# A decoder trunk's first layer: the norm's column product on another engine, low parts and sines issued later, the first weights split elsewhere

## The chip, the cores and the metric

The kernel runs on one core of a Trainium2 chip. The metric is the device time of one execution in microseconds (us). The core has TensorE (PE, with its weight loads PEld), VectorE (DVE), ScalarE (ACT), GpSimd (POOL) and SyncE (SP), which here only issues DMA transfers. Each engine works through its own queue in order and waits on semaphores for what others produce.

## What is computed

Two layers of a decoder trunk over 512 tokens and 2048 channels. The part that matters here is the head of a layer: a modulation vector from `c`, an RMS norm of `x`, and one large projection.

```python
for l in range(DEPTH):
    mod = c_act @ ada_w[l] + ada_b[l]
    shift, scale, gate = [m[:, None, :] for m in jnp.split(mod, 3, axis=-1)]
    h = rms_norm(x, norm_g[l]) * (1.0 + scale) + shift
    z = h @ w_in[l]
    ...                      # attention and conv groups from z's columns, cos/sin tables for the rope
    x = x + gate * y
```

## The kernel before

Tokens lie along the free axis; channels along the 128 partitions, in 16 chunks of 128 channels by 512 tokens. All matmuls are fp32 made of two fp32r parts: a value is split into a high part (a rounding cast) and a low part (the difference), and `mm3` (L248 to L251) issues three matmuls, high x high, high x low, low x high. Weights are split by `split_w` (L235): the cast on ScalarE (L242), the difference on the engine that is named (L243; `SENG`, GpSimd). A load of eight 128x128 weight tiles (`load_w`, L228, four buffers "raw") is cut into two such splits of 128x512, each with 5 buffers for high and low.

**The start.** `rope_angles` makes angles on VectorE. `first_x` (L373) loads x and sums its squares: squares on ScalarE, additions on VectorE (the first on GpSimd), and at the end two additions that join three partial sums (L384, L385). `token_rsqrt` (L212 on) sums over channels on TensorE (L194) and takes the inverse root on VectorE in a chain of small steps (L215, L176 to L184), and `token_bc` (L204, L209) spreads it over the partitions. `rope_tables` (L168) takes two sines on ScalarE.

**The modulation.** `Gemv.block(l, b)` (L332) makes 128 columns of the modulation: it loads a 1 MB block of `ada_w` into one of three buffers ("ada") and VectorE multiplies and reduces it (L336, 128x2048). Block j is the shift of chunk j (called shift block j below), block 16 + j its scale (scale block j). `make_gs` (L348, L350) turns the scale into (1 + scale) * norm_g, a 128x1 step on VectorE. `make_h` (L352) then makes h of a chunk in three steps: x * gs * rstd on VectorE (L356), the high part with the shift added on ScalarE (L357), the low part on VectorE (L358).

**Layer 0's order.** `modulated(j)` (L422) is, in the program's order: scale block j (for j = 0 it is done earlier, `EARLY` = 1), L350, shift block j, L356, L357, L358. `chunk` (L397) loads eight weight tiles and gives TensorE 24 matmuls for one chunk of h. There are three passes: chunks 0 to 2 of the first projection (`K1` = 3; the sums in PSUM are then parked, copies L431), 8 chunks of the gate's columns with h 0 to 7 (`KH`; parked too), and chunks 3 to 15 of the first projection. `modulate_to` (L434) keeps h ahead of TensorE: 0.6 chunks of h for each chunk of weights in the second pass, 0.7 in the third. What follows (attention, conv, output, layer 1) is not touched.

**What sets the order.** The program is traced in the order above, and a planner then orders each engine's queue: of the instructions that it believes ready at a time it takes the one that was traced first. `issue_after` puts what a block traces behind one instruction on that engine, `keep_in_program_order` (the GpSimd splits) behind the one before. The DMA queue's order on SP is that of the program in this stage. A load into a buffer waits at the head of SP's queue until the buffer is free, and the loads behind it wait too.

Of the kernel before, what the change touches and what calls it, by code (L numbers as in the profile page):

```python
# [50 lines left out]
def hybrid_trunk(ctx, tc, xT, c, pos, invf, vec, adaT, w_s, w_t, w_kr, w_q, w_kv, w_pw, w_o, outT):  # L51
# [287 lines left out]
    def shift(l, j):  # L339
        return mods[l][:, j:j + 1]  # L340
# [11 lines left out]
    def make_h(l, j, x, rstd, h=None, tk=slice(0, S)):  # L352

        h = r4("h") if h is None else h
        hi, lo, x = h[:, 0, tk], h[:, 1, tk], x[:, tk]
        V.scalar_tensor_tensor(out=x, in0=x, scalar=gs(l, j), in1=rstd, op0=ALU.mult, op1=ALU.mult)  # L356
        A.activation(out=hi, in_=x, func=AF.Identity, bias=shift(l, j))  # L357
        bc_ins[1] = V.scalar_tensor_tensor(out=lo, in0=x, scalar=shift(l, j), in1=f(hi), op0=ALU.add,  # L358
                                           op1=ALU.subtract)
        return h  # L360
# [12 lines left out]
    def first_x():  # L373
        xs = []
        accs = [ms("acc") for _ in range(3)]
        for j in range(0, KC, 2):
            t = r4f("x")
            nc.sync.dma_start(out=t, in_=xT[j:j + 2].rearrange("k p t -> p k t"))
            for e in range(2):

                acc = accs[2] if j < 4 else accs[e]
                square_sum(acc, t[:, e], j + e if j < 4 else j - 4, nc.gpsimd if j < 4 else V)
                xs.append(t[:, e])
        V.tensor_add(out=accs[0], in0=accs[0], in1=accs[2])  # L384
        V.tensor_add(out=accs[0], in0=accs[0], in1=accs[1])  # L385
        return xs, accs[0]

    def layer(l, xs, rstd, rpsum):
# [5 lines left out]

        tags = [t for t in ("mm", "up", "s", "cv", "pz") for _ in range(NB[t])]

        def chunk(tiles, src, hj, start, stop):  # L397
            raw = load_w(src, 8, P)
            for q in (0, 4):
                hi, lo = split_w(raw[:, q:q + 4], SENG)  # L400
                for n in range(4):
                    mm3(tiles[q + n], hi[:, n], lo[:, n], hj[:, 0], hj[:, 1], start, stop)

# [15 lines left out]

        h, part = [], [None] * H  # L420
        if l == 0:
            def modulated(j):  # L422
                if j >= EARLY:
                    scale0(j)
                g.block(0, j)
                h.append(make_h(0, j, xs[j], rstd if j else rpsum[0]))

            def park(tiles, where):
                for n in range(8):
# [1 line left out]
                    (A.copy if n % 2 else V.tensor_copy)(out=p, in_=tiles[n])  # L431
                    yield p

            def modulate_to(m):  # L434
                while len(h) < min(int(m), KC):
                    if len(h) < NI:
                        with tc.issue_after(rstd_ins.ins):
                            modulated(len(h))
                    else:
                        modulated(len(h))  # L440

            first = [psum(t, "z") for t in tags]
            for j in range(K1):
                modulate_to(j + 1)
                chunk(first, w_first(j), h[j], j == 0, j == K1 - 1)
            held = list(park(first, lambda n: ms("held") if n < 2 else f2("held", "held", 6, sp)))
            mg = [psum(t, "z") for t in tags]
            for j in range(KH):
                modulate_to(max(j + 1, K1 + MR0 * (j + 1)))
                chunk(mg, w_t[l, 0:H, :, j, :].rearrange("a p b -> p a b"), h[j], j == 0, j == KH - 1)  # L450
            part = list(park(mg, lambda n: ms("part")))
            first = [psum(t, "z") for t in tags]
            for j in range(K1, KC):
                modulate_to(max(j + 1, K1 + MR0 * KH + MR * (j + 1 - K1)))
                chunk(first, w_first(j), h[j], j == K1, j == KC - 1)
            krw = kr_weights()
            for n in range(8):
# [570 lines left out]

    def scale0(j):
        g.block(0, 16 + j)  # L1030
        make_gs(0, j)

    for j in range(EARLY):
        scale0(j)
    rstd0 = ms("rstd")
    state = (xs, rstd0, [token_rsqrt_bc(acc, D, rstd0)])
    rope_tables()
    rstd_ins = bc_ins[0]
    for l in range(DEPTH):
        state = layer(l, *state)  # L1040
# [61 lines left out]
```

## Time and profile before

| | us |
|---|---|
| median of 3 runs | 1679.31 |
| lowest, highest | 1675.61, 1680.39 |
| the profiled execution | 1681.96 |
| its span | 1680.2 |
| TensorE busy in the span | 1587.6 |
| VectorE busy | 1211.6 |
| ScalarE busy | 687.5 |
| GpSimd busy | 640.5 |

The profile is one execution. Its span runs from the first instruction to the last; the execution's own time is 1.8 us longer. Times below are us from the span's start, the mean of one instruction in ns. In the name of a step, `ada` is a modulation block, `mod` the modulation columns, `h` a chunk of h, `hi` and `lo` the parts of weights, `raw` loaded weights, `z` the projection's sums in PSUM. The engine named behind an arrow is the one that released a waiting instruction.

### The profile page before, as it was taken

The page shows a single profiled execution, that of the slowest core. Times are in us where ns is not written, and L with a number is a line of the kernel's source. Part 1 is how long each engine was busy: PE and PEld are TensorE (multiplying, and loading weights), DVE is VectorE, ACT ScalarE, POOL GpSimd, SP SyncE. Part 2 cuts the span into 40 slices and gives each one's busy share as a digit, 9 for nine tenths or more (in the row PEclk, how much of TensorE's full clock was granted, in tenths as well). Part 3 has the DMA queues.
Part 4 walks back from the last instruction along what each step waited for, and adds up shares of the span by engine and source line. Part 5 has one row for each costly group of instructions (what it writes and reads, how often), then busy time and mean ns, then how long its engine had stood idle before and what let it go on. Part 6 is the DMA issues. An engine that isn't in the chain of part 4 may idle for free.

```text
span 1680.2 us, 20681 instructions
## 1 busy us (share of the span) xinstructions
PE 1587.6 (94%) x7350; PEld 1299.3 (77%) x7350; DVE 1211.6 (72%) x2008; ACT 687.5 (41%) x1284; POOL 640.5 (38%) x440
## 2 busy tenths in 40 slices
PE   4988999999999999998899899999999999999999
PEld 2766778887878888877678678888787878888888
DVE  8898897888899645665469856677887786555553
ACT  4222455554544345321223355544544443532221
POOL 3565633424233445554535546243343326200000
PEclk9999999999999999999999999999999999999999
DMA  8878323222232732797885633233223335337672
GB/s 299 281 282 290 132 86 97 68 84 82 76 108 84 238 100 89 254 331 268 307 293 181 267 97 104 72 98 97 75 71 97 105 128 181 93 110 253 237 261 88
DMA packets 82890, 271.53 MB, mean 162 GB/s; under 512 B 10721, under 2 KB 21729, under 8 KB 70241
## 3 DMA queue, kind: packets, MB, share of 16 engines
q1 hardware_dynamic: 82786, 270.20, 47.5%
q8 instruction: 58, 0.95, 0.2%
q14 instruction: 46, 0.38, 0.1%
HBM read 257.55 MB, written 12.62 MB: 161 GB/s over the span
## 4 chain that ended last, share of the span: by engine, by line
PE 55%; DVE 27%; DMA 6%; ACT 6%; issue 3%; POOL 1%; SPq 0%; POOLq 0%; DVEq 0%; ACTq 0%
DVE ada L336 7%; DVE cv L547 7%; PE wo L251 4%; PE z L251 4%; PE z L249 4%; PE z L250 4%; PE wo L249 4%; PE wo L250 4%; PE cg L251 3%; PE cg L249 3%; PE cg L250 3%; DMA ada<-in_adaT_dram 3%; DMA raw<-in_w_o_dram 3%; PE pw L250 2%; PE pw L251 2%
## 5 line engine op out<-in xcount | busy, mean ns | idle before, releaser
L243 POOL TENSOR_TENSOR lo<-raw,hi 128x512 fp32r<-128x512 f32 x380 | 575.6, 1530 | 690.1 <-ACT hi L242 680.9
L242 ACT CAST hi<-raw 128x512 fp32r<-128x512 f32 (+1 forms) x512 | 306.4, 612 | 559.3 <-PE wo L250 152.9
L547 DVE SCALAR_TENSOR_TENSOR cv<-u,lvec,cv 128x512 f32<-128x512 f32 x464 | 348.7, 751 | 7.2
L249 PE MATMUL z<-h,hi 128*128 128x512 f32 (+1 forms) x782 | 308.2, 399 | 17.0 <-ACT h L357 10.9
L251 PE MATMUL z<-h,lo 128*128 128x512 f32 (+1 forms) x782 | 308.7, 395 | 8.6 <-POOL lo L243 8.5
L250 PE MATMUL z<-h,hi 128*128 128x512 f32 (+1 forms) x782 | 307.2, 393 | 0.7 <-DVE h L358 0.7
L336 DVE CUSTOM_DVE_ANT_0 ada<-ada,cb,avec 128x2048 f32<-128x2048 f32 x96 | 251.2, 2618 | 27.3 <-DMA ada<-in_adaT_dram 27.3
L249 PE MATMUL wo<-cat,hi 128*128 128x512 f32 (+1 forms) x544 | 207.8, 382 | 11.0 <-ACT hi L242 10.9
L251 PE MATMUL wo<-cat,lo 128*128 128x512 f32 (+1 forms) x544 | 207.9, 382 | 4.2 <-POOL lo L243 3.8
L250 PE MATMUL wo<-cat,hi 128*128 128x512 f32 (+1 forms) x544 | 207.0, 381 | 0.0
L249 PEld LDWEIGHTS z<-h,hi 128*128 128x128 f32 x782 | 150.0, 193 | 49.2 <-ACT h L357 13.4
L251 PEld LDWEIGHTS z<-h,lo 128*128 128x128 f32 x782 | 149.9, 192 | 43.3 <-POOL lo L243 13.5
L250 PEld LDWEIGHTS z<-h,hi 128*128 128x128 f32 x782 | 149.8, 192 | 29.5 <-DVE h L358 1.8
L243 DVE TENSOR_TENSOR lo<-raw,hi 128x512 fp32r<-128x512 f32 (+1 forms) x132 | 85.5, 660 | 80.3 <-ACT hi L242 80.1
L249 PEld LDWEIGHTS wo<-cat,hi 128*128 128x128 f32 x544 | 103.8, 191 | 32.0 <-ACT hi L242 13.1
L251 PEld LDWEIGHTS wo<-cat,lo 128*128 128x128 f32 x544 | 103.6, 190 | 26.3 <-POOL lo L243 6.8
L250 PEld LDWEIGHTS wo<-cat,hi 128*128 128x128 f32 x544 | 103.8, 191 | 19.0
L249 PE MATMUL cg<-h,hi 128*128 128x512 f32 x256 | 101.0, 394 | 0.0
L251 PE MATMUL cg<-h,lo 128*128 128x512 f32 x256 | 99.8, 390 | 0.0
L250 PE MATMUL cg<-h,hi 128*128 128x512 f32 x256 | 99.8, 390 | 0.0
L780 ACT ACTIVATE pr<-pr,smx,sc 128x128 f32<-128x128 f32 (+1 forms) x64 | 41.9, 654 | 110.3 <-DVE smx L779 110.2
L251 PE MATMUL mg<-h,lo 128*128 128x512 f32 x192 | 76.3, 397 | 2.3 <-POOL lo L243 2.3
(265 smaller groups left out, 2469.4 us busy)
## 6 DMA issues: line engine op xcount, KB each, us to landing
ada<-in_adaT_dram SPq DMA_DIRECT2D x96, 1024.0 KB, 5.5
raw<-in_w_t_dram SPq DMA_DIRECT2D x120, 512.0 KB, 3.9
raw<-in_w_o_dram SPq DMA_DIRECT2D x64, 512.0 KB, 5.8
raw<-in_w_s_dram SPq DMA_DIRECT2D x32, 512.0 KB, 6.4
raw<-in_w_pw_dram SPq DMA_DIRECT2D x16, 512.0 KB, 3.6
raw<-in_w_q_dram SPq DMA_DIRECT2D x24, 256.0 KB, 2.7
x<-in_xT_dram SPq DMA_DIRECT2D x8, 512.0 KB, 7.3
kf<-kfd SPq DMA_DIRECT2D x16, 256.0 KB, 3.9
```

What stands on the lines that cost most here:

```text
L242: A.copy(out=hiv, in_=rawv)
L243: i = eng.tensor_tensor(out=lov, in0=rawv, in1=f(hiv), op=ALU.subtract)
L249: T.matmul(out=ps, lhsT=whi, rhs=mhi, start=start, stop=False)
L250: T.matmul(out=ps, lhsT=whi, rhs=mlo, start=False, stop=False)
L251: T.matmul(out=ps, lhsT=wlo, rhs=mhi, start=False, stop=stop)
L336: V.tensor_tensor_reduce(out=t, in0=t, in1=self.cb, scale=1.0, scalar=vv(l, "ada_b", b), op0=ALU.mult, op1=ALU.add, accum_out=mods[l][:, b ...
L547: V.scalar_tensor_tensor(out=box[-1], in0=u[:, k:k + S], scalar=w, in1=box[0], op0=ALU.mult, op1=ALU.add)
L780: A.activation(out=pr[:, :n], in_=pr[:, :n], func=AF.Exp, scale=scl, bias=nb, accum_out=sums)
```

## The change

- `make_gs` for layer 0 becomes an activation on ScalarE: gs = scale * norm_g + norm_g, with norm_g as both the scale and the bias column.
- The low part of a chunk (L358) is no longer traced right behind its high part. It is held in `pending` and traced behind the next chunk's scale block: either when the next chunk is modulated, or at once where the chunk is the last that was made and TensorE is about to use it; then the next scale block is begun first (`begin(j + 1)`), except for chunk 0.
- The sines are traced behind the high part of chunk 0 instead of before the layer.
- The first chunk's weights are split on VectorE instead of GpSimd.
- The addition L384 is traced behind the fifth load of x instead of at the end.

```diff
@@ first_x
-        V.tensor_add(out=accs[0], in0=accs[0], in1=accs[2])
+            if j == 8:
+                V.tensor_add(out=accs[0], in0=accs[0], in1=accs[2])
         V.tensor_add(out=accs[0], in0=accs[0], in1=accs[1])
@@ layer
-        def chunk(tiles, src, hj, start, stop):
+        def chunk(tiles, src, hj, start, stop, eng=SENG):
...
-                hi, lo = split_w(raw[:, q:q + 4], SENG)
+                hi, lo = split_w(raw[:, q:q + 4], eng)
...
+            pending, begun = [], [EARLY]
+
+            def begin(j):
+                if j < KC and j == begun[0]:
+                    begun[0] += 1
+                    scale0(j)
+
+            def settle():
+                while pending:
+                    pending.pop()()
+
             def modulated(j):
-                if j >= EARLY:
-                    scale0(j)
+
+                begin(j)
+                settle()
                 g.block(0, j)
-                h.append(make_h(0, j, xs[j], rstd if j else rpsum[0]))
+                t, r = r4("h"), rstd if j else rpsum[0]
+                hi, lo, x = t[:, 0], t[:, 1], xs[j]
+                V.scalar_tensor_tensor(out=x, in0=x, scalar=gs(0, j), in1=r, op0=ALU.mult, op1=ALU.mult)
+                hi_ins[0] = A.activation(out=hi, in_=x, func=AF.Identity, bias=shift(0, j))
+                pending.append(lambda: V.scalar_tensor_tensor(out=lo, in0=x, scalar=shift(0, j), in1=f(hi),
+                                                              op0=ALU.add, op1=ALU.subtract))
+                h.append(t)
...
-            def modulate_to(m):
+            def modulate_to(m, j):
...
+                if j == len(h) - 1 and pending:
+                    if j:
+                        begin(j + 1)
+                    settle()
...
             for j in range(K1):
-                modulate_to(j + 1)
-                chunk(first, w_first(j), h[j], j == 0, j == K1 - 1)
+                modulate_to(j + 1, j)
+                if j == 0:
+                    with tc.issue_after(hi_ins[0].ins):
+                        rope_tables()
+                chunk(first, w_first(j), h[j], j == 0, j == K1 - 1, SENG if j else V)
...
     def scale0(j):
         g.block(0, 16 + j)
-        make_gs(0, j)
+        n = vv(0, "norm_g", j)
+        A.activation(out=gs(0, j), in_=gs(0, j), func=AF.Identity, scale=n, bias=n)
...
-    rope_tables()
```

## Rows read from the trace of the kernel before

**Rows 1.** Table by stretch: busy us (count) of PE, PEld, DVE, ACT, POOL, clock, DMA, GB/s.
```profile
104.00:190.60 86.60, 78.86 (x322) 62.07 (x323) 75.32 (x64) 24.31 (x44) 52.61 (x29) 0.96 0.69 251
120.00:130.00 10.00, 10.00 (x46) 8.29 (x45) 9.17 (x6) 1.75 (x3) 6.50 (x5) 1.00 0.71 252
```

**Rows 2.** Chain of waits in the first 420 us, shares by engine and line.
```profile
by line: DVE ada L336 18.3%; DVE cv L547 7.2%; PE z L251 5.1%; issue 5.1%; PE z L249 5.0%; PE z L250 4.8%; DVE x L356 4.2%; DVE mod L350 3.2%; DVE h L358 2.4%; ACT h L357 2.3%; DVE lat L586 2.0%; PE st L194 1.6%; DVE pr L776 1.4%; DMA raw<-
```

**Rows 3.** Groups of DVE, 43.6 to 185.9 us: count | busy us, mean ns | idle before.
```profile
L336 DVE CUSTOM_DVE_ANT_0 ada<-ada,cb,avec 128x2048 f32<-128x2048 f32 x28 | 81.1, 2896 | 0.0
L356 DVE SCALAR_TENSOR_TENSOR x<-x,mod,rstd 128x512 f32<-128x512 f32 x14 | 19.5, 1393 | 0.4
L350 DVE SCALAR_TENSOR_TENSOR mod<-mod,avec 128x1 f32<-128x1 f32 x14 | 13.7, 978 | 0.4
```

**Rows 4.** Groups of POOL, 43.6 to 188 us, the weights' low parts.
```profile
L243 POOL TENSOR_TENSOR lo<-raw,hi 128x512 fp32r<-128x512 f32 x44 | 87.4, 2013 | 61.8 <-ACT hi L242 61.8
```

**Rows 5.** Timeline of DVE: start, duration, step [idle before, releaser].
```profile
110.78 0.15 DVE L350 SCALAR_TENSOR_TENSOR mod<-mod,avec 128x1 f32<-128x1 f32 x1
...
135.99 0.75 DVE L358 SCALAR_TENSOR_TENSOR h<-x,mod,h 128x512 fp32r<-128x512 f32 x1 [0.79 <-ACT h L357]
136.66 2.34 DVE L336 CUSTOM_DVE_ANT_0 ada<-ada,cb,avec 128x2048 f32<-128x2048 f32 x1
...
139.04 1.09 DVE L350 SCALAR_TENSOR_TENSOR mod<-mod,avec 128x1 f32<-128x1 f32 x1
140.17 1.74 DVE L356 SCALAR_TENSOR_TENSOR x<-x,mod,rstd 128x512 f32<-128x512 f32 x1
141.83 2.34 DVE L336 CUSTOM_DVE_ANT_0 ada<-ada,cb,avec 128x2048 f32<-128x2048 f32 x1
...
144.97 0.75 DVE L358 SCALAR_TENSOR_TENSOR h<-x,mod,h 128x512 fp32r<-128x512 f32 x1 [0.79 <-ACT h L357]
```

**Rows 6.** Timeline of POOL in the same stretch (x6, x4: splits in one run).
```profile
111.06 12.92 POOL L243 TENSOR_TENSOR lo<-raw,hi 128x512 fp32r<-128x512 f32 x6 [3.82 <-ACT hi L242]
...
138.00 3.36 POOL L243 TENSOR_TENSOR lo<-raw,hi 128x512 fp32r<-128x512 f32 x2 [5.88 <-ACT hi L242]
145.52 7.57 POOL L243 TENSOR_TENSOR lo<-raw,hi 128x512 fp32r<-128x512 f32 x4 [4.16 <-ACT hi L242]
```

**Rows 7.** Waits, 20 to 200 us: total us, times, longest.
```profile
DVE h L358 <- ACT h L357: 11.9, 15, 0.8
```

**Rows 8.** Timeline of DVE at the start, chunk 0.
```profile
22.33 0.69 DVE L384 TENSOR_TENSOR acc<-acc,acc 128x512 f32<-128x512 f32 x1
...
23.66 2.34 DVE L336 CUSTOM_DVE_ANT_0 ada<-ada,cb,avec 128x2048 f32<-128x2048 f32 x1
...
26.05 1.09 DVE L350 SCALAR_TENSOR_TENSOR mod<-mod,avec 128x1 f32<-128x1 f32 x1
...
27.13 1.23 DVE L176 TENSOR_SCALAR sm<-sm 128x4 int32<-128x4 int32 x1
...
33.32 0.75 DVE L356 SCALAR_TENSOR_TENSOR x<-x,mod,stb 128x512 f32<-128x512 f32 x1 [0.58 <-ACT rstd L222]
33.98 2.35 DVE L336 CUSTOM_DVE_ANT_0 ada<-ada,cb,avec 128x2048 f32<-128x2048 f32 x1
...
36.25 1.76 DVE L358 SCALAR_TENSOR_TENSOR h<-x,mod,h 128x512 fp32r<-128x512 f32 x1
```

**Rows 9.** Timelines of PE, POOL and ACT at the start.
```profile
23.80 1.86 PE L194 MATMUL st<-ones,acc 128*128 128x1 f32 x8 [9.22 <-DVE acc L385]
24.53 3.81 POOL L243 TENSOR_TENSOR lo<-raw,hi 128x512 fp32r<-128x512 f32 x2 [10.27 <-ACT hi L242]
42.26 0.72 ACT L357 ACTIVATE h<-x,mod 128x512 fp32r<-128x512 f32 x1 [6.41 <-DVE mod L336]
```

**Rows 10.** Timeline of SP's queue (x2: two issues, the second waits).
```profile
126.16 5.18 SPq L335 DMA_DIRECT2D ada<-in_adaT_dram  x2
```

**Rows 11.** DMA issues to 200 us (KB, median us to landing); weights' landings to 60 us.
```profile
ada<-in_adaT_dram SPq DMA_DIRECT2D x32, 1024.0 KB, 5.1
...
DMA to landing us min/median/max: 5.8/6.5/12.1
```

More of the change, by code (lines that the diff above doesn't have):

```diff
@@ L421, in layer @@
         if l == 0:
+            pending, begun = [], [EARLY]
[6 more added lines that the diff above has]
+                    pending.pop()()
             def modulated(j):
-                if j >= EARLY:
-                    scale0(j)
+                begin(j)
+                settle()
                 g.block(0, j)
-                h.append(make_h(0, j, xs[j], rstd if j else rpsum[0]))
+                t, r = r4("h"), rstd if j else rpsum[0]
[5 more added lines that the diff above has]
+                h.append(t)
+            hi_ins = [None]
             def park(tiles, where):
@@ L448, in layer @@
             for j in range(KH):
-                modulate_to(max(j + 1, K1 + MR0 * (j + 1)))
+                modulate_to(max(j + 1, K1 + MR0 * (j + 1)), j)
                 chunk(mg, w_t[l, 0:H, :, j, :].rearrange("a p b -> p a b"), h[j], j == 0, j == KH - 1)
@@ L453, in layer @@
             for j in range(K1, KC):
-                modulate_to(max(j + 1, K1 + MR0 * KH + MR * (j + 1 - K1)))
+                modulate_to(max(j + 1, K1 + MR0 * KH + MR * (j + 1 - K1)), j)
                 chunk(first, w_first(j), h[j], j == K1, j == KC - 1)
```

## The prediction

> **What bounds the kernel now.** I read the chain of waits first, to see which engine ends last while layer 0 makes its h. VectorE's column products (L336, "blocks" below) lead it, and the small steps around them (L356, L350, L358) follow [rows 2]. The table by stretch agrees: in the last pass over the first projection TensorE is busy for 78.9 of 86.6 us and VectorE for 75.3 [rows 1], but TensorE is fed, not full. Where it never waits it starts 46 matmuls in 10 us, 0.217 each [rows 1]; a chunk of 24 is 5.2 us, and the 13 chunks of that pass 68 us, 18 us less than it took. So the stage ends when VectorE has made h 15, plus one chunk, and everything after it starts from there.
>
> VectorE's timeline shows one chunk: scale block 2.34, L350, L356, shift block (as long as the scale block), a wait of 0.79 for ScalarE's high part (L357), low part 0.75 [rows 5]. There are 15 such waits, 11.9 us in all [rows 7].
>
> What L350 really costs is the point where readers go wrong. Its mean is 978 ns [rows 3] for a 128x1 product. But at 110.78, just before GpSimd starts at 111.06, it took 0.15; at 139.04, with GpSimd working since 138.00, it took 1.09 [rows 5, 6]. L356 likewise is 0.75 at 33.32 and 1.74 at 140.17 [rows 5, 8]. Each weight split on GpSimd holds the next VectorE instruction up by about 1 us, whichever that is. From the grouped rows: 28 blocks x (2.896 - 2.34) = 15.6, 14 x (0.978 - 0.15) = 11.6, 14 x (1.393 - 0.75) = 9.0, together 36.2 us for 44 splits [rows 3, 4, 5], 0.82 a split. The splits stay, so L350's excess does not go with L350; it falls on the next instruction.
>
> The Trainium skill says so too: "SBUF — State Buffer", SBUF: two separate sides, has VectorE and GpSimd share a port pair under an exclusive lock, with the loser fully blocked. By that rule 14 x 0.98 = 13.7 us must not be booked as gained, only the 0.15 each; the rows above agree.
>
> **Part by part.** The sum is made on the profiled execution (span 1680.2 us, its own time 1681.96, so 1.8 lie around the span). The median of the runs is 1679.31, 2.65 lower; I take the gain off the median.
>
> *Norm's product on ScalarE.* Removed: 0.15 a chunk on VectorE. No row shows a 128x1 activation with two column operands; at most it is L357's 0.72 for 128x512 [rows 9], and at the least it costs nothing. Both ends are hidden: between its input (scale block) and its reader (L356) the shift block's 2.34 now stands, since L356 comes behind both blocks. In exchange L356 no longer overlaps anything in front of the high part. Free of GpSimd, a chunk before is 2.38 (scale block to L350) + 0.13 + 0.67 + 3.14 (shift block and wait) + 0.67 = 6.99 start to start, from rows 5 with 1.0 of GpSimd's taken off 139.04 and off 140.17; after it is 2.38 + 2.38 + 1.54 (L356, L357, hops) + 0.67 = 6.97. So zero, to 0.13 x 15 = 2.0.
>
> *Low part behind the next block.* In the program the scale block of j+1 now precedes low part j. But the planner orders each engine by what it believes ready, and the program's order breaks ties only. It did that before: scale block 1 went in front of low part 0 (33.98 against 36.25 [rows 8]), though it stands behind it in the program. In the other chunks it left the 0.79 empty, with a block's data long there in the trace: issued at 126.16, some 5.1 us to landing, run at 136.66 [rows 5, 10, 11]. So the planner believes those data late, later than the low part's input, and nothing in the change brings them sooner where a weight load stands between two chunks' blocks in SP's queue. Only for chunks 1, 2 and 7 does the change issue the next scale block directly behind this chunk's shift block, ahead of the weight load. I take those three waits as gone, 3 x 0.79 = 2.4, less 1.4, because after chunks 2 and 7 the parked copies lose the block that now fills their gaps (2 x 0.7): +1.0. Bounds: -0.5 (TensorE's matmuls with h's low part start a block later there) and, all 15 gone, 11.3.
>
> *Where the splits fall.* Before, in a run of four splits (145.52 [rows 6]) VectorE met them with scale block, L350, L356 and shift block. After it has scale block, shift block, L356 and then the wait for the high part, which costs nothing when a split sits in it. Five runs have four or more splits; 5 x 0.82 = 4.1 us. Bounds: 0, if longer blocks between the splits push the fourth past the wait, and 4.1.
>
> *Start.* The first weights split on VectorE removes GpSimd's 24.53 to 28.34 [rows 9], beside which L350 took 1.09 and L176 1.23 instead of some 0.15 each: 2.0 off the path to the first L356. The early addition takes up to 0.69 (22.33 [rows 8]) off the end of the square sums, and the sines leave ScalarE; 0.3 taken, since VectorE's additions follow one another there. Against that: scale block 0 (23.66, 2.34) lies exactly over TensorE's sums (23.80, 1.86) [rows 8, 9]. With the sums earlier the planner may start the steps behind them first; then VectorE stands idle for those 1.86 and the block comes later. Bounds at the first L356: +0.4 to +2.3; I take 0.4, as the block's data come no sooner while the sums do. From there to high part 1 before: 33.32 to 42.26, 8.9 us. After: L356 0.67, one split 0.62 (the other fits into the 0.58 that L356 waits), two blocks 4.7, low part 0.67, L356 0.75, one split of GpSimd in the way 1.0: 8.4. Gain 0.5 (-0.6 with both splits in the way, 1.5 without GpSimd's).
>
> *Sines later.* Two activations on ScalarE behind high part 0, some 1.1 us in which ScalarE has only the casts of weights 1 to make, needed when high part 1 comes, some 8 us on [rows 9]; the tables' first reader is behind the projections. Nothing.
>
> *The queues.* SP: weights 1 now wait behind scale block 2, whose buffer comes free when shift block 0 is done, where the old order tied them to a buffer free one block earlier; weights 2 likewise behind scale block 3. From the end of shift block 0 (33.32 at the latest) to high part 1 (42.26) are 8.9 us [rows 8, 9]; a landing takes 6.5 in the median [rows 11]. GpSimd has two splits less, nothing waits.
>
> Sum: 0 + 1.0 + 4.1 + 0.4 + 0.5 = 6.0 us at h 15, and on to the end, as nothing behind it is tied to absolute time. **1679.3 - 6.0 = 1673.3, say 1673.**
>
> **Rivals.**
> - *All low parts move* (B). If the planner does keep the program's order, 11.3 us of waits and 2.0 of L350 go, copies give 1.4 back, the start gives 0.9, and the splits find no wait any more (two were absorbed before, -1.7): 11.1, at most 14 with the better start: 1668 to 1665. For: the change names that order. Against: the 0.79 that stayed empty.
> - *Nothing measurable* (C). As forecast, but the fourth split misses the wait (-4.1) or TensorE, waiting longer for low part 2 and 7, hands its losses on: gain 2, 1677. For: TensorE's idle in the last pass is paced by more than VectorE. Against: 18 us of slack there.
> - *Slower* (D). ScalarE's queue is in order. If the casts of weights 1 and 2 stand in front of high parts 1 and 2 and the loads land at the slowest landing seen, 12.1 us, instead of 6.5 [rows 11], each holds the high part back for some 5 us, and L356 and both blocks behind it: -10 + 6 = 4 to 6 us lost, 1684. It decides from landings of about 8.2 us, when weights arrive after the high part's input. Against: one landing of that length, at the crowded start.
> - *The product's microsecond is its own* (E). Then 14 x 0.83 = 11.6 more, 1661. Against: 0.15 at 110.78.
>
> **How the numbers follow.** Forecast 0.50, B 0.18, C 0.21, D 0.08, E 0.03. Some 0.3%, 5 us, is what a measurement of this kernel can tell from no change. The forecast's own range is 1670 to 1677 (terms at their bounds, 2 to 9 us), so about 0.6 of its chance is beyond 0.3%: 0.30 + 0.18 + 0.03 + 0.02 of C = 0.53 faster; 0.20 + 0.17 + 0.01 = 0.38 same; 0.09 slower. The range reaches to B's better start and into C's far side: 1664 to 1680.
>
> **What would show it.** VectorE's order: low part j in front of scale block j+1 with 0.79 before it (forecast), or behind it without (B). L350's line gone, but the blocks' mean above 2.9 us instead of 2.896, with the lost microseconds on them. High part 1 some 1 us earlier than 42.26 and high part 15 some 6 us earlier than before. L176 back near 0.15. Scale block 0 in front of L215 or between the small steps. The prediction is wrong if TensorE's idle before L249 and L251 in the last pass grows, or if the stretches after 190 us change their length.

## The result, and the profile after

The median of six runs is 1669.0 us (1664.9 to 1673.4), against 1681.7 for the kernel before in the same comparison: ratio 0.9933, 95% interval 0.9911 to 0.9955, some 11.3 us less. The forecast was 1673, faster, range 1664 to 1680: the direction and the range held, the gain is nearly twice the 6.0 us of the sum. The kernel before was slower in this comparison than in the three runs that the forecast started from (1679.3). The profiled execution took 1673.4 us with a span of 1671.5.

One mark serves as a gauge below: the start of ScalarE's high part of a chunk, which VectorE's work ends in. High part 1 started at 42.26 us before [rows 9] and starts at 39.50 now; high part 15, the last, at 184.48 before and 171.81 now.

```profile
184.48 0.72 ACT L357 ACTIVATE h<-x,mod 128x512 fp32r<-128x512 f32 x1 [7.32 <-DVE mod L336]
171.81 0.73 ACT L442 ACTIVATE h<-x,mod 128x512 fp32r<-128x512 f32 x1 [3.09 <-DVE mod L336]
```

A mark also holds by how much the execution was early or late ahead of the change. VectorE's additions of the squares (L370), which everything here waits for, begin at 15.76 us before and at 15.21 now; in the four executions whose start is the unchanged one they begin between 14.93 and 15.76. So 0.55 us of both differences need not be the change's.

The stretch that corresponds to the first line of [rows 1], from the table by stretch (columns as there): TensorE's busy share rose from 0.91 to 0.95.

```profile
95.00:180.30 85.30, 80.68 (x337) 63.37 (x336) 72.60 (x62) 30.51 (x59) 66.83 (x33) 0.98 0.75 277
```

VectorE's groups from 41 to 173.2 us, to be laid beside [rows 3] (count | busy us, mean ns | idle before):

```profile
L336 DVE CUSTOM_DVE_ANT_0 ada<-ada,cb,avec 128x2048 f32<-128x2048 f32 x28 | 87.1, 3111 | 0.0
L441 DVE SCALAR_TENSOR_TENSOR x<-x,mod,rstd 128x512 f32<-128x512 f32 x14 | 15.2, 1089 | 5.0 <-ACT mod L1060 5.0
L443 DVE SCALAR_TENSOR_TENSOR h<-x,mod,h 128x512 fp32r<-128x512 f32 x15 | 13.9, 928 | 9.9 <-ACT h L442 9.9
```

L350's line is gone, 13.7 us. L336 became longer (2896 to 3111 ns), L356, now L441, shorter (1393 to 1089), and L441 has a wait of its own in front, 11 times, that the kernel before did not have. From the table of waits, beside [rows 7]:

```profile
DVE h L443 <- ACT h L442: 9.9, 14, 0.8
DVE x L441 <- ACT mod L1060: 5.0, 11, 0.5
```

Two chunks in VectorE's timeline, beside [rows 5] (start, duration, step, [idle before, releaser]):

```profile
130.81 0.75 DVE L441 SCALAR_TENSOR_TENSOR x<-x,mod,rstd 128x512 f32<-128x512 f32 x1 [0.46 <-ACT mod L1060]
131.48 3.38 DVE L336 CUSTOM_DVE_ANT_0 ada<-ada,cb,avec 128x2048 f32<-128x2048 f32 x1
...
135.66 0.89 DVE L443 SCALAR_TENSOR_TENSOR h<-x,mod,h 128x512 fp32r<-128x512 f32 x1 [0.79 <-ACT h L442]
136.48 3.38 DVE L336 CUSTOM_DVE_ANT_0 ada<-ada,cb,avec 128x2048 f32<-128x2048 f32 x1
...
140.32 1.23 DVE L441 SCALAR_TENSOR_TENSOR x<-x,mod,rstd 128x512 f32<-128x512 f32 x1 [0.46 <-ACT mod L1060]
141.48 3.38 DVE L336 CUSTOM_DVE_ANT_0 ada<-ada,cb,avec 128x2048 f32<-128x2048 f32 x1
...
145.66 0.90 DVE L443 SCALAR_TENSOR_TENSOR h<-x,mod,h 128x512 fp32r<-128x512 f32 x1 [0.79 <-ACT h L442]
```

and GpSimd's, beside [rows 6]:

```profile
131.37 4.65 POOL L243 TENSOR_TENSOR lo<-raw,hi 128x512 fp32r<-128x512 f32 x2 [3.83 <-ACT hi L242]
136.21 9.80 POOL L243 TENSOR_TENSOR lo<-raw,hi 128x512 fp32r<-128x512 f32 x4 [0.20 <-ACT hi L242]
```

Three things are to be seen. The order is scale block, L441, shift block, low part, next scale block: the low part stayed in front of the next block, and L441 stayed in front of the shift block. The wait of 0.46 before L441 is for ScalarE's product (0.39 us, third row below). And the splits lie elsewhere: the pair of 131.37 meets the shift block of 131.48, which takes 3.38 instead of 2.34, and then the wait of 0.79 with the low part behind it, which takes 0.89 instead of 0.75. In the kernel before the pair of 138.00 held up L350 and L356, one microsecond each [rows 5, 6], and the wait of 0.79 stood empty. So a chunk with two splits takes 8.47 us from high part to high part now (126.43 to 134.90), against 8.98 before (135.23 to 144.21), more often 9.06 (in the second pass, where one of the two still meets L441, it takes 8.80 and 8.96 now); one with four takes 10.00 (134.90 to 144.90) against 11.07 (144.21 to 155.28).

ScalarE's timeline shows why the splits moved: the weights' casts (L242), which release the splits, stand behind the product in its queue.

```profile
39.50 0.72 ACT L442 ACTIVATE h<-x,mod 128x512 fp32r<-128x512 f32 x1 [3.21 <-DVE mod L336]
...
126.43 0.72 ACT L442 ACTIVATE h<-x,mod 128x512 fp32r<-128x512 f32 x1 [3.09 <-DVE mod L336]
130.39 0.39 ACT L1060 ACTIVATE mod<-mod,avec 128x1 f32<-128x1 f32 x1 [3.24 <-DVE mod L336]
130.68 1.12 ACT L242 CAST hi<-raw 128x512 fp32r<-128x512 f32 x2
134.90 0.73 ACT L442 ACTIVATE h<-x,mod 128x512 fp32r<-128x512 f32 x1 [3.10 <-DVE mod L336]
```

The start in VectorE's timeline, beside [rows 8]:

```profile
24.80 0.16 DVE L215 TENSOR_SCALAR sm<-st 128x4 f32<-128x4 f32 x1 [1.96 <-PE st L194]
...
25.13 2.35 DVE L336 CUSTOM_DVE_ANT_0 ada<-ada,cb,avec 128x2048 f32<-128x2048 f32 x1
...
31.65 1.29 DVE L243 TENSOR_TENSOR lo<-raw,hi 128x512 fp32r<-128x512 f32 x2
32.86 0.74 DVE L441 SCALAR_TENSOR_TENSOR x<-x,mod,stb 128x512 f32<-128x512 f32 x1
...
36.45 0.75 DVE L441 SCALAR_TENSOR_TENSOR x<-x,mod,rstd 128x512 f32<-128x512 f32 x1
37.12 2.35 DVE L336 CUSTOM_DVE_ANT_0 ada<-ada,cb,avec 128x2048 f32<-128x2048 f32 x1
```

Scale block 0 went behind L215, which waited 1.96 us for the sums. Both splits of the first weights fit in front of the first L441. Then L441 of chunk 1 (36.45) runs ahead of shift block 1 (37.12), and no split of GpSimd lies in between.

### The profile page after: what moved, and what is told of

It is laid out like the page before. It is cut to its first block, busy times and chain, and to the rows that moved or that the text cites. A ratio compares the mean times of both kernels' runs of the same rounds, so it can differ in the third digit from the quotient of the medians.

```text
span 1671.5 us, 20673 instructions
## 1 busy us (share of the span) xinstructions
PE 1586.9 (95%) x7350; PEld 1300.0 (78%) x7350; DVE 1203.0 (72%) x1994; ACT 692.6 (41%) x1300; POOL 650.8 (39%) x438
## 4 chain that ended last, share of the span: by engine, by line
PE 56%; DVE 26%; DMA 7%; ACT 6%; issue 3%; POOL 2%; SPq 0%; POOLq 0%; DVEq 0%; ACTq 0%
DVE ada L336 7%; DVE cv L575 7%; PE z L251 5%; PE z L250 5%; PE z L249 5%; PE wo L251 5%; PE wo L249 4%; PE wo L250 4%; PE cg L251 3%; PE cg L250 3%; PE cg L249 3%; DMA raw<-in_w_o_dram 3%; DMA ada<-in_adaT_dram 2%; PE pw L250 2%; PE pw L251 2%
## 5 line engine op out<-in xcount | busy, mean ns | idle before, releaser
L243 POOL TENSOR_TENSOR lo<-raw,hi 128x512 fp32r<-128x512 f32 x378 | 586.2, 1566 | 670.6 <-ACT hi L242 653.5
L242 ACT CAST hi<-raw 128x512 fp32r<-128x512 f32 (+1 forms) x512 | 306.5, 611 | 551.8 <-PE wo L250 155.1
L336 DVE CUSTOM_DVE_ANT_0 ada<-ada,cb,avec 128x2048 f32<-128x2048 f32 x96 | 258.8, 2699 | 30.8 <-DMA ada<-in_adaT_dram 30.7
```

The lines of the kernel that those rows point to most:

```text
L242: A.copy(out=hiv, in_=rawv)
L243: i = eng.tensor_tensor(out=lov, in0=rawv, in1=f(hiv), op=ALU.subtract)
L336: V.tensor_tensor_reduce(out=t, in0=t, in1=self.cb, scale=1.0, scalar=vv(l, "ada_b", b), op0=ALU.mult, op1=ALU.add, accum_out=mods[l][:, b ...
```

## The experiments

Theory T1: GpSimd's split holds up VectorE's next instruction by a microsecond unless VectorE happens to wait there, and the change gained by giving it waits in the right places. Rivals: T2, the low parts' new order made the gain; T3, the start did; E, VectorE simply has less to do, and a new wait is plain loss. The marks of all runs (us; the ratio is to the kernel before; "squares" is the start of L370's first addition):

| kernel | ratio, 95% | squares | high part 1 | high part 15 | 1 to 15 |
|---|---|---|---|---|---|
| before | | 15.76 | 42.26 | 184.48 | 142.22 |
| after | 0.9933, 0.9911 to 0.9955 | 15.21 | 39.50 | 171.81 | 132.31 |
| after, product back on VectorE | 0.9965, 0.9947 to 0.9982 | 15.40 | 39.98 | 180.78 | 140.80 |
| before, product on ScalarE | 0.9934, 0.9916 to 0.9952 | 14.93 | 40.13 | 172.51 | 132.38 |
| before, start's edits | 1.0008, 0.9995 to 1.0022 | 15.17 | 41.83 | 185.60 | 143.77 |
| before, low part's order | 0.9983, 0.9968 to 0.9998 | 15.19 | 39.59 | 180.62 | 141.03 |
| after, low parts behind the block | 0.9872, 0.9851 to 0.9894 | 15.34 | 39.63 | 166.63 | 127.00 |
| after, addition last | 0.9897, 0.9877 to 0.9917 | 15.29 | 37.47 | 169.77 | 132.30 |
| after, no product | 0.9923, 0.9897 to 0.9949 | 15.05 | 39.33 | 173.50 | 134.17 |
| after, longer wait | 0.9924, 0.9898 to 0.9949 | 15.43 | 39.83 | 173.66 | 133.83 |
| after, low parts behind and addition last | 0.9890, 0.9865 to 0.9916 | 15.98 | 38.16 | 165.15 | 126.99 |
| the same, splits on VectorE | 0.9828, 0.9801 to 0.9856 | 15.05 | 37.23 | 152.18 | 114.95 |
| before, splits on VectorE | 0.9831, 0.9805 to 0.9858 | 15.47 | 38.33 | 155.37 | 117.04 |
| after, splits on VectorE | 0.9853, 0.9837 to 0.9869 | 15.54 | 39.82 | 159.07 | 119.25 |

A ratio is known to 2 to 5 us either way. The marks come from one execution each and show where the time went; a mark moves with the start of the squares by up to 1 us, the last column does not: kernels that differ only ahead of high part 1 agree there within 0.01 us (132.31 and 132.30, 127.00 and 126.99). What follows high part 15 took 1487.7 to 1503.4 us in these fourteen executions, so a mark and a time can differ by several microseconds.

### The product back on VectorE, in the kernel after

```diff
     def scale0(j):
         g.block(0, 16 + j)
-        n = vv(0, "norm_g", j)
-        A.activation(out=gs(0, j), in_=gs(0, j), func=AF.Identity, scale=n, bias=n)
+        make_gs(0, j)
```

> The kernel after, with one part undone: the 128x1 product of norm and scale goes back to VectorE, everything else of the change stays. Theory T1 (collisions absorbed): each GpSimd split holds up VectorE's next instruction by about 1 us, and what the product's move bought is that VectorE now waits 0.46 us for ScalarE there, time in which a split goes by without holding anything up; the product back on VectorE takes 1 us from row to row again (it took 0.98 us on the mean in the kernel before), 14 times less 11 waits of 0.46: 14 x 0.98 - 5.0 = 8.7 us of the gain of 11.3 are lost, so about 1677 to 1678, and the wait for ScalarE's product is gone. Rival T2 (the low parts' order made the gain): about 1669 to 1671, as the kernel after. Rival T3 (the start made it): about 1670 too, with the last chunks' high parts no later than now.

1676.2 us: by the ratios 5.9 us of the gain of 11.3 are left, so about half is lost. By the marks it is more: the last high part is 9.0 us later than in the kernel after, 8.5 of it between high parts 1 and 15 (140.80 less 132.31), where T1 had 8.7. VectorE's groups there (columns as above): the product takes 1126 ns, and the wait before L441 is gone.

```profile
L441 DVE SCALAR_TENSOR_TENSOR x<-x,mod,rstd 128x512 f32<-128x512 f32 x14 | 18.5, 1319 | 0.5
L350 DVE SCALAR_TENSOR_TENSOR mod<-mod,avec 128x1 f32<-128x1 f32 x14 | 15.8, 1126 | 0.4
```

### The product alone, in the kernel before

```diff
     def scale0(j):
         g.block(0, 16 + j)
-        make_gs(0, j)
+        n = vv(0, "norm_g", j)
+        A.activation(out=gs(0, j), in_=gs(0, j), func=AF.Identity, scale=n, bias=n)
```

> The kernel before, with one part of the change alone: the 128x1 product on ScalarE. T1: the chunks' period falls as in the kernel after, from the second chunk on; about 8 to 9 us faster than before (1672 to 1673), high part 1 still near 42 us in the profile, the last high part near 175 to 176 us. Rival T2: 0 to 2 us faster, since the low parts stand where they stood. Rival T3: 0 to 1 us faster.

1669.8 us: this one line brings the whole of the change's gain. High part 15 comes 11.97 us earlier than before, 9.84 of it between high parts 1 and 15. T1 had expected some 9 and high part 1 unchanged. Of the other 2.1, 0.83 is the execution's (squares from 14.93 against 15.76), and 1.27 was gained from high part 0 to high part 1 (8.16 before, 6.89 here), where a split now meets the wait of 0.79 instead of L350. L350's 1.09 at 26.05 [rows 8] brought nothing: the same pair of splits holds up two of the next small steps in its place (0.16 each in the kernel before), and from L384 to the first L356 it is 10.96 us against 10.99.

```profile
26.28 1.19 DVE L182 TENSOR_TENSOR sm<-sm 128x4 f32<-128x4 f32 x1
27.50 1.18 DVE L183 TENSOR_TENSOR sm<-sm 128x4 f32<-128x4 f32 x1
```

T2 and T3 fall as causes of the steady gain.

### The start's edits alone

```diff
-        V.tensor_add(out=accs[0], in0=accs[0], in1=accs[2])
+            if j == 8:
+                V.tensor_add(out=accs[0], in0=accs[0], in1=accs[2])
...
-                chunk(first, w_first(j), h[j], j == 0, j == K1 - 1)
+                if j == 0:
+                    with tc.issue_after(hi_ins[0].ins):
+                        rope_tables()
+                chunk(first, w_first(j), h[j], j == 0, j == K1 - 1, SENG if j else V)
...
-    rope_tables()
```

> The kernel before, with the start's edits alone: the early addition of the sums, the sines behind the first high part, the first weights split on VectorE. T3: high part 1 starts near 39.5 to 40 us (42.26 before) and all later ones stay that much earlier, 2.3 to 2.8 us faster (about 1678). T1 says the same, for this part is no collision of the steady stretch. If instead the early gain is given back at the next wait for weights, the last high part stands where it stood (184.5 us) and the time is that of before.

No change in time (1.0008). High part 1 comes 0.43 us earlier, not 2.3 to 2.8, and the squares began 0.59 earlier, so that nothing is left of it: weights 1 are split from 35.42, as before, and still hold up low part 0 and L350. Between high parts 1 and 15 it takes 1.55 us longer. VectorE waits longer for TensorE there where it parks the first sums, 2.75 us in all (0.96 and 0.21 in the kernel before):

```profile
54.10 0.69 DVE L433 COPY held<-z 128x512 f32<-128x512 f32 x1 [1.75 <-PE z L251]
55.79 0.69 DVE L433 COPY held<-z 128x512 f32<-128x512 f32 x1 [1.00 <-PE z L251]
```

High part 15 is 1.1 us later than before. What the kernel after gained at high part 1 was thus not the start's edits.

### The low part's order alone

The kernel before with `pending`, `begin` and `settle` of the change, and nothing else of it:

```diff
             def modulated(j):
-                if j >= EARLY:
-                    scale0(j)
+                begin(j)
+                settle()
                 g.block(0, j)
...
+                if j == len(h) - 1 and pending:
+                    if j:
+                        begin(j + 1)
+                    settle()
```

> The kernel before, with one part of the change alone: a chunk's low part is issued once the next chunk's block has begun. T1: the order on VectorE changes at chunk 1 alone, all other low parts stay in front of the next scale block; 0 to 1 us faster (1679 to 1682). Rival T2: most of the 11.3 us, about 1670 to 1673, with the waits for ScalarE's high part (0.8 us, 14 to 15 times) gone or fewer.

0.9983: 2.9 us, hardly above nothing. On VectorE low part 1 alone changed its place, as T1 had it. But high part 1 comes 2.67 us earlier (2.10 counted from the squares), from the queue of loads: weights 1 stand behind scale block 2 there, so that GpSimd begins to split them at 40.90 instead of 35.41, when high part 1 is done.

```profile
40.90 3.77 POOL L243 TENSOR_TENSOR lo<-raw,hi 128x512 fp32r<-128x512 f32 x2 [13.13 <-ACT hi L242]
```

### The price of a wait: no product, and a longer one

Two kernels that change the wait of 0.46: the first leaves ScalarE's product out, the second makes ScalarE work longer. Both also move the casts that stand behind the product.

```diff
     def scale0(j):
         g.block(0, 16 + j)
-        n = vv(0, "norm_g", j)
-        A.activation(out=gs(0, j), in_=gs(0, j), func=AF.Identity, scale=n, bias=n)
```

> The kernel after with the product of norm and scale left out altogether (X takes the scale column as the block leaves it; norm's gain and the 1 added to scale are missing from what is computed). VectorE runs X straight behind the scale block: its 11 waits of 0.46 us (5.0 us) go and no work is added. Theory T1: the splits that those waits let by then hold up X and its neighbours; X rises from 1.09 us on the mean towards 1.4 to 1.8, and the time is within 2 us of the kernel after. Rival E (the product's move gained because VectorE has less to do, and the new wait is plain loss): 5 us faster than the kernel after, about 1664.

```diff
         A.activation(out=gs(0, j), in_=gs(0, j), func=AF.Identity, scale=n, bias=n)
+        A.activation(out=gs(0, j), in_=gs(0, j), func=AF.Identity)
```

> The kernel after with one more ScalarE instruction, a copy of the 128x1 product onto itself, behind each product: VectorE's wait for it grows by about 0.39 us, 11 to 16 times, nothing else changes. Rival E (a wait is plain loss): 4.3 to 6.2 us slower than the kernel after. T1: the longer wait lets more of a split by, and costs less than half of that, 0 to 2.5 us.

With no wait at all the ratio is 0.9923, with the longer one 0.9924, against 0.9933 with 0.46: neither the waits taken away nor those added show in the time, which could hardly tell 5 us here. By the marks both kernels are slightly slower between high parts 1 and 15 than the kernel after, 1.9 and 1.5 us, where E had 5 us faster and 4 to 6 slower. (The second instruction took 0.20 us, not 0.39, so the waits grew by 3.5 us in all, and E's share shrinks to that.) The waits before L441 make 0.5, 5.0 and 8.5 us in all in "no product", the kernel after and "longer wait", and L441's mean is 1661, 1089 and 1090 ns. One L441 that met a split in each, from the timelines of "no product" and of "longer wait" (that of the kernel after stands above, at 140.32: 0.46 and 1.23):

```profile
149.72 1.65 DVE L441 SCALAR_TENSOR_TENSOR x<-x,mod,rstd 128x512 f32<-128x512 f32 x1
```

```profile
141.93 1.00 DVE L441 SCALAR_TENSOR_TENSOR x<-x,mod,rstd 128x512 f32<-128x512 f32 x1 [0.69 <-ACT mod L1061]
```

L441 undisturbed is 0.75. Its excess and the wait in front of it make 0.90 + 0, 0.48 + 0.46 and 0.25 + 0.69: 0.90, 0.94 and 0.94. The low part behind its wait of 0.79 makes 0.15 + 0.79 = 0.94 again. So where a split is due, VectorE loses some 0.94 us whatever the wait in front of it is, up to the longest here, 0.79. Two rows of "longer wait" are outside this: L441 takes 1.87 us at 53.63 and at 102.44 behind waits of 0.47 and 0.46. And where no split is due a wait is plain loss, as E says: in 5 of the kernel after's 11 waits L441 takes 0.75 behind it, as at 130.81, and "longer wait" makes such a chunk 8.70 us (127.58 to 136.28) instead of 8.47. E falls as the account of the whole: the waits that were taken away, 4.5 us in all, made the kernel no faster.

The pair also splits the 8.5 us that lie between "product back" and the kernel after. Leaving the product out brings 6.6 of them (140.80 to 134.17), three times its own 14 x 0.15 = 2.1; the wait, and the casts that stand behind it, bring 1.9 more (134.17 to 132.31). T1 as I had stated it gave the wait the whole; it is the smaller part. A chunk with four splits took 11.1 with the product on VectorE and takes 9.8 to 10.0 in "no product" and 10.0 in the kernel after: the fourth split meets the wait of 0.79 now. A chunk with two takes 8.8 to 9.0 in "no product" (8.82 from 127.08 to 135.90) and 8.47 only with the product, whose wait itself lets nothing by there: the casts behind it bring the pair to the shift block and to the wait of 0.79.

### Low parts behind the next block

```diff
+                    if len(h) > 1 and begun[0] > len(h):
+                        with tc.issue_after(sc_ins[0].ins):
+                            pending.pop()()
+                    else:
+                        pending.pop()()
-                    pending.pop()()
...
-        g.block(0, 16 + j)
+        sc_ins[0] = g.block(0, 16 + j)
```

> The kernel after, with every low part from chunk 1 on placed behind the next chunk's scale block on VectorE, where the change's words put it and its order does not have it: scale block, low part of the chunk before, X, shift block. The 14 waits of 0.7 to 0.8 us for ScalarE's high part (9.9 us) and the 11 waits of 0.46 for its product (5.0) go. Theory T1 (a split holds up VectorE's next instruction unless VectorE waits at that moment): GpSimd's 46 splits then find VectorE never idle and cost about 0.9 to 1.0 us each, 41 to 46 us in the place of 29.0; net 14.9 less 12 to 17, so within 3 us of the kernel after. Rival (waits are plain loss, collisions stay 0.63 us a split): 12 to 15 us faster at the last high part, some 11 at the end.

1661.9 us. High part 15 comes 5.2 us earlier than in the kernel after: outside T1's 3, far from the rival's 12 to 15. Both waits are gone, and the rows say what came for them:

```profile
L336 DVE CUSTOM_DVE_ANT_0 ada<-ada,cb,avec 128x2048 f32<-128x2048 f32 x28 | 81.9, 2953 | 0.0
L447 DVE SCALAR_TENSOR_TENSOR h<-x,mod,h 128x512 fp32r<-128x512 f32 x15 | 22.5, 1502 | 0.8 <-ACT h L446 0.8
L445 DVE SCALAR_TENSOR_TENSOR x<-x,mod,rstd 128x512 f32<-128x512 f32 x14 | 21.7, 1553 | 0.0
```

Excess over the undisturbed 2.345, 0.745 and 0.745: 28 x 0.608 + 15 x 0.757 + 14 x 0.808 = 39.7 us. In the kernel after the same sum is 28 x 0.766 + 14 x 0.344 + 15 x 0.183 = 29.0. So 14.1 us of waits went and 10.7 of collisions came, 3.4 net; the rest to 5.3 was not traced. T1's mechanism holds: 39.7 us are 0.88 for each of the 45 splits in that stretch. Its sum was off because it took 46 of them at 0.9 to 1.0. The time says less: by the ratios the whole kernel gains some 10 us over the kernel after, near the rival's 11, but of the 11.2 us between the two profiled executions 6.0 lie behind high part 15, where nothing was changed.

### The addition back at the end

```diff
-            if j == 8:
-                V.tensor_add(out=accs[0], in0=accs[0], in1=accs[2])
+        V.tensor_add(out=accs[0], in0=accs[0], in1=accs[2])
         V.tensor_add(out=accs[0], in0=accs[0], in1=accs[1])
```

> The kernel after, with the addition of the first two sums back behind the last square. It asks whether the sums' new order is what put scale block 0 behind the small steps (1.96 us of idle VectorE before them). If so, scale block 0 is done before the sums' row arrives, as in the kernel before, and the first X starts 0 to 1.9 us earlier; all later high parts follow by as much, and the time is that of the kernel after less 0 to 1.9 us.

Scale block 0 runs over the sums again, and L215 no longer waits:

```profile
22.64 2.35 DVE L336 CUSTOM_DVE_ANT_0 ada<-ada,cb,avec 128x2048 f32<-128x2048 f32 x1
24.91 0.16 DVE L215 TENSOR_SCALAR sm<-st 128x4 f32<-128x4 f32 x1
...
30.22 0.75 DVE L440 SCALAR_TENSOR_TENSOR x<-x,mod,stb 128x512 f32<-128x512 f32 x1
```

High part 1 and high part 15 both come 2.0 us earlier than in the kernel after; the ratio says 0.9897 against 0.9933, with intervals that overlap a little. By the marks the early addition cost the change 2 us.

The two edits together:

> The kernel after with both edits that made it faster one by one: every low part from chunk 1 on behind the next scale block, and the addition of the first two sums back behind the last square. Alone they put the last high part 5.2 us (171.81 to 166.63) and 2.0 us (171.81 to 169.77) earlier. If the two lie on different stretches (the chunks, the start), they add: last high part at 164.6 us, 7 us under the kernel after, about 1660. If TensorE or the weights' DMAs bind the chunks by now, the 2 us of the start are given back at a later chunk: last high part at 166 to 167.

High part 15 at 165.15 where 164.6 was expected (its squares began 0.64 later than in the kernel with low parts behind the block), so both add; its time (1662.7) cannot be told from that of low parts behind the block alone.

### The splits on VectorE

```diff
-        def chunk(tiles, src, hj, start, stop):
+        def chunk(tiles, src, hj, start, stop, eng=SENG):
...
-                hi, lo = split_w(raw[:, q:q + 4], SENG)
+                hi, lo = split_w(raw[:, q:q + 4], eng)
...
-                chunk(first, w_first(j), h[j], j == 0, j == K1 - 1)
+                chunk(first, w_first(j), h[j], j == 0, j == K1 - 1, V)
```

and the same V in the two other loops over chunks: in the version with both edits, in the kernel before, and in the kernel after.

> The kernel of the run before in this list (low parts behind the next block, addition last) with all splits of the first pass on VectorE (0.61 to 0.69 us each, as the two first ones in the kernel after) instead of GpSimd. If a GpSimd split costs VectorE about 1.0 us there, as the rows with low parts and X at 1.77 instead of 0.75 say, and four splits on GpSimd fill a 10.0 us chunk by themselves, the chunks with two splits fall from 7.9 to about 7.2 us and those with four from 10.0 to about 8.3: 44 splits times 0.35 = 15 us at most at the last high part, less where TensorE (busy 0.95 and 0.97 of these stretches) or the DMAs (0.92, 0.82) bind next; 4 to 10 us expected. If the held-up instructions are not GpSimd's doing, VectorE has 44 x 0.65 = 29 us more to do and the time rises by up to as much.

> The kernel before with nothing changed but the engine of the first pass's splits: VectorE instead of GpSimd. It measures the price that the prediction put on a split's collision. If VectorE's excess over its undisturbed times (36.2 us, 44 splits times 0.82) is GpSimd's doing, the scale and shift blocks all take 2.34 us, the product 0.15, X and low part 0.75, and 44 splits of 0.61 to 0.69 us are added, some of them in the waits of 0.79 us for the high part: 36 less 27 to 30 at the least, plus up to 9 in those waits, so 6 to 16 us faster at the last high part, some 1665 to 1675. If the excess has another cause, it stays, and the kernel is up to 30 us slower.

> The kernel after with nothing changed but the engine of the first pass's splits: VectorE instead of GpSimd, as was done with the kernel before in the run ahead of this one (last high part 155.37 us, ratio 0.9831). It asks what the change is worth where GpSimd holds nothing up. If its 11.3 us are collisions let by in waits (T1), nearly nothing is left of them there: only the product's own 0.15 us, 14 times, about 2 us, less the waits that it adds; last high part between 152 and 157 us, ratio within 0.003 of 0.983. If the change has a worth of its own, independent of GpSimd, the last high part comes some 10 us earlier than 155.37, ratio about 0.977.

The kernel before gains 28 us from the engine's name alone (1654.2 us, high part 15 at 155.37, 29.1 earlier), more than the 6 to 16 expected. VectorE's groups, columns as above:

```profile
L336 DVE CUSTOM_DVE_ANT_0 ada<-ada,cb,avec 128x2048 f32<-128x2048 f32 x28 | 65.7, 2345 | 0.0
L243 DVE TENSOR_TENSOR lo<-raw,hi 128x512 fp32r<-128x512 f32 x42 | 27.0, 684 | 0.0
L356 DVE SCALAR_TENSOR_TENSOR x<-x,mod,rstd 128x512 f32<-128x512 f32 x14 | 10.5, 751 | 0.4
L358 DVE SCALAR_TENSOR_TENSOR h<-x,mod,h 128x512 fp32r<-128x512 f32 x15 | 11.2, 744 | 0.0
```

Every block is back at 2345 ns L356 at 751 and L350 at 158: the whole excess of [rows 3] was GpSimd's doing. The waits for the high part are gone too, since the splits fill them. 36 us of collisions and 11.9 of waits went, 27.0 of splits came: 21 of the 25.2 us between high parts 1 and 15. The parked copies' waits for TensorE fell from 2.4 to 0.6, 1.8 more; 3.9 came ahead of high part 1, 0.29 of it from earlier squares. The expectation had up to 9 us for the waits and left out the last two.

In the kernel after the same edit leaves high part 15 at 159.07, 3.7 later than in the kernel before with it, 2.2 of that between high parts 1 and 15, and the ratio is 0.9853 against 0.9831. So the change is worth nothing where GpSimd is silent, by the marks less than nothing (the ratios cannot tell the two apart): waits of 3.2 us for the product and 2.4 for the high part remain, which here let nothing by. Expected was a last high part of 152 to 157.

The version with both edits is the fastest by the marks (152.18) and level with the kernel before with this edit by the time (1653.2 and 1654.2). It had been expected 4 to 10 us ahead of the same with GpSimd's splits; between high parts 1 and 15 it was 12.0 (126.99 to 114.95). The table by stretch of the former, columns as in [rows 1], shows VectorE, the DMA engines and TensorE all near their full share in the first stretch and TensorE never idle in the second; which of them binds was not tested.

```profile
45.00:90.00 45.00, 43.95 (x193) 36.05 (x193) 44.92 (x56) 18.79 (x36) 0.00 (x0) 1.00 1.01 356
90.00:155.00 65.00, 65.00 (x288) 53.81 (x288) 62.94 (x76) 23.64 (x43) 0.00 (x0) 1.00 0.85 325
```

## Why the prediction was right, and where it was not

- *VectorE bounds the stage, and the pass ends a chunk after h 15.* Right. The first addition of parked sums, which waits for the pass, came 11.75 us earlier (188.01 to 176.26), high part 15 12.7 earlier, the kernel by its ratio 11.3. The prediction's sign of being wrong did not show in the last pass: TensorE was idle for 7.7 us in the first line of [rows 1] and for 4.6 in its counterpart. What follows 188.01 and 176.26 took 1492.2 and 1495.2 us, a change of 3.0 that is within the spread of executions given above.
- *A split holds up the next VectorE instruction by some 1 us, so L350's mean is not to be booked.* Right, and shown: with the splits on VectorE L336 is 2345 ns. So is that the excess of L350 falls on others: from "product back" to "no product" L350 goes with 13.7 us of excess, and the collisions on all instructions fall by 4.1 only (39.5 to 35.4, summed as for the low parts behind the block). The product on ScalarE then brings them to 29.0, for 4.5 us of new waits. Rival E, which booked 13.7 us for the product, is refuted by "no product": 6.6. Rival C's gain of 2 lies outside the interval of the ratio, 8 to 15 us.
- *The number.* 1669.0 lies outside the forecast's own 1670 to 1677 and inside the stated range only through what that range allowed for the better rivals. That it held is luck in part: the two largest misses below, 4.4 us on the product with the splits and 1.8 on the way to high part 1, went the same way.

The terms of the sum beside what the marks give (us earlier at high part 15; what the parts brought in the chunks is read between high parts 1 and 15, the first two lines from "product back" to the kernel after by way of "no product"):

| term | forecast | measured |
|---|---|---|
| product, and where the splits fall | 0 + 4.1 | 6.6 + 1.9 |
| low part behind the next block | 1.0 | 1.4 |
| start, to the first L356, counted from the squares | 0.4 | -0.1 |
| from there to high part 1 | 0.5 | 2.3 |
| sum | 6.0 | 12.1 |

With the 0.55 us by which the squares began earlier this makes the 12.7 of the marks.

- *Product, 0 to 2.0.* The sum put L356 behind both blocks, so that the shift block would hide ScalarE's product. That step failed: L356 stayed in front of the shift block, 11 waits of 0.46 came, and the product's own 0.15 a chunk, which the sum had set off against that, is 2.1 of the 6.6. Without GpSimd that makes a chunk longer, not level: with all splits on VectorE the change costs 2.2 us between high parts 1 and 15.
- *Where the splits fall, 4.1 (0 to 4.1).* The mechanism was right: a split that meets a wait costs nothing, and the fourth of a run meets the 0.79 now. With the product's 2.1 it makes 6.2, and 6.6 was measured (4.1 of it collisions). What the sum lacked is the other 1.9: ScalarE's product also moves the casts, and so the splits, to where chunks with two splits let one by. It had no wait before L356 and so no such place.
- *Low part behind the next block, +1.0.* Right that the planner would leave it in front of the block; it moved chunk 1's alone, not those of 2 and 7. Before to "product back" is 1.4 us between high parts 1 and 15, the order alone 1.2. Rival B's order, made by force, did give about B's time (1661.9; B had 1665 to 1668), though not by B's sum: B had 11.3 us of waits go and 1.7 of collisions come. Counted from the kernel before, as B did, 11.1 went (11.9 to 0.8) and 3.5 came (36.2 to 39.7), and high part 15 came 17.9 earlier, where B had 14 at most.
- *Start, +0.4 (0.4 to 2.3).* Right in its rows, not in size: scale block 0 went behind L215, which waited 1.96, and L176 is back at 0.17, as foreseen. The first L356 did come 0.46 us earlier (33.32 to 32.86), but that is luck: the squares began 0.55 earlier, and from there to the first L356 it is 17.65 us against 17.56. The sum had put one of VectorE's two splits behind that step; both stand in front of it (31.65). With the addition back the same stretch takes 14.93, 2.6 less than before, more than the upper bound.
- *From there to high part 1, +0.5 (-0.6 to 1.5).* Missed: 8.94 became 6.64, 2.3 us, outside the bounds. The sum had put one split of VectorE (0.62) and one of GpSimd (1.0) in the way. There was neither; of the latter the queue of loads is the reason: weights 1 were issued at 32.14 instead of 26.42, behind scale block 2, and their split began at 40.81 instead of 35.41. The prediction saw that order in SP's queue and asked only whether it would be late. For a split, late was good.
- *The queues, 0, and rival D.* The weights' landings to 60 us took 7.0, 10.2 and 12.1 us (least, median, most) against 6.5 in the median before [rows 11], beyond D's point of 8.2 in the median; high part 1 was not held up by them: ScalarE waited 3.21 us for the shift block there.

## What to carry to other kernels

Ask of every wait on an engine whether another engine's work goes by in it: here waits of 0.46 to 0.79 us cost nothing in front of an instruction that a split was due to hold up, and their whole length where none was. When a group's mean is far above its undisturbed duration, find the engine that causes it and cost that engine's work elsewhere: 44 splits of 0.68 us on VectorE were 28 us cheaper than the same on a GpSimd that had time to spare. And where a load is moved, ask what its landing triggers, not only whether it is in time.

## What was not expected of the hardware

- A 128x512 split on GpSimd costs VectorE some 0.9 to 1.1 us, be the held instruction a 128x1 product (0.15 to 1.09), a 128x512 step (0.75 to 1.65) or a block (2.34 to 3.38), though GpSimd's own rows show 2.3 us for it (4.65 for two at 131.37). The Trainium skill ("SBUF — State Buffer", SBUF: two separate sides) says that a VectorE instruction with two inputs in SBUF and a GpSimd instruction that reads SBUF lock each other out: the one that starts first holds the shared ports for its whole instruction while the other blocks. The trace agrees in that the price hardly depends on what is held up; that the rest of GpSimd's 2.3 is its own waiting for VectorE would fit the rule, and was not measured by itself.
- With four splits in a chunk GpSimd hardly pauses: 9.80 us from 136.21, behind 0.20 of idle time. Such a chunk took 10.0 us in the kernel after, with the longer wait and with the low parts behind the block alike, so that there GpSimd rather than VectorE seems to set the pace; no run tested that by itself.
- An activation of a 128x1 column with columns for scale and bias took 0.39 us on ScalarE (130.39), the one without such columns in "longer wait" 0.20.
